# Seven block products in place of eight in the down projection of 12 of 16 feature groups, interleaved with the up projection

## The chip, the cores and the metric

One NeuronCore of one Trainium2 chip runs the whole program. The metric is the device time of one execution in microseconds; smaller is better. TensorE is called PE here (with PEld for its weight loads), VectorE DVE, ScalarE ACT, GpSimd POOL and SyncE SP.

## The reference, cut to what matters

The program is a decoder trunk of two layers on 256 tokens with 1024 model features, in float32. In each layer three attention branches are mixed and added to the residual stream x; that part is not touched. Then follows the MLP with 4096 hidden features:

```
h2 = RMSNorm(x, g_mlp)
x  = x + square(relu(h2 @ w_up)) @ w_down      # w_up 1024 x 4096, w_down 4096 x 1024
```

At the end stands a final RMSNorm of x.

## The kernel before, in words

**Numbers in two parts.** A float32 matrix product is made of three products of a shorter float format (float32r). Each operand is split into a high part (an ACT copy into that format) and a low part (a DVE subtraction, original minus high part, both inputs in SBUF). `split` (lines 84 to 93) does so for weights, with four buffers for each part (`whi`, `wlo`), 128x1024 at a time. `mm3` (117 to 121) issues the three matmuls high-high, high-low, low-high into one PSUM tile.

**Weights.** Every weight block comes by a DMA of 1 MB from the SP queue into one of four buffers `raw`, then goes through two splits. `w_cols` (111) brings 256 columns of all 1024 rows, `w_rows` (99) 512 rows of 512 columns.

**The MLP (665 to 726).** The 4096 hidden features are 16 groups of 256. The norm's factor per token is left out of the up product and put in at the end as its square (`r2`).
The up stage runs over the groups: for each of the two blocks of 128 features, eight steps over the model features, three matmuls each, with a weight block as the stationary operand and all 256 tokens as the moving one: 48 matmuls of 256 columns per group. Then `up_done` makes relu (ACT, from PSUM), the square (DVE, `max(o,0) * r`, one input from PSUM), the high part (ACT) and the low part (DVE), and the group stays in SBUF as `uh`, `ul` (a pair of tiles for each group).
The down stage runs after all 16 groups: `stream_tok` makes for each half of the output columns (`cg`, 512 columns) 32 steps over the hidden features, for each of the two token blocks `j`, three matmuls of 512 columns with an activation block 128x128 as the stationary operand. A group of 256 features takes 2 steps x 2 token blocks x 2 halves = 8 block products, 24 matmuls. The result in PSUM is scaled by r2 and added to x by DVE (line 713).
In layer 0 the transposes of x for the next layer's norm (`norm_in`, `part`) follow each half; in layer 1 the final norm and the output DMAs.

**Order.** PE's order is written out by hand from the attention output projection to the first two up groups (`tc.manual_schedule`, left at line 694). Everything else, on every engine, is put in order at build time by a planner that follows its own timing of the program; on the chip each engine then runs its list strictly in order, and an instruction that waits holds up those behind it. POOL has no work in the MLP but a few tiny operations for the norm.

**PSUM** has eight banks: three under the name mm, two at, two pt, one av.

Of the kernel before, what the change touches and what calls it, by code (L numbers as in the profile page):

```python
# [32 lines left out]
def trunk_kernel(ctx: ExitStack, tc: tile.TileContext, x, positions, g_mix, w_in, b_forget, w_branch,  # L33
                 w_out, g_mlp, w_up, w_down, g_final, out):
    nc = tc.nc
    act, dve, pool, pe, dma = nc.scalar, nc.vector, nc.gpsimd, nc.tensor, nc.sync
# [7 lines left out]
    def mm_tile(name="mm"):  # L44
        return ps.tile([128, 512], F32, name=name, tag="mm", bufs=3)
# [4 lines left out]
    def pt_tile(name="pt"):  # L50
        return ps.tile([128, 512], F32, name=name, tag="pt", bufs=2)
# [6 lines left out]
    xs = [[xh[h][:, j, :] for h in range(2)] for j in range(2)]  # L58
# [21 lines left out]
    mhalf = const.tile([128, 2], F32, name="mhalf")  # L80
    pool.memset(mhalf, -0.5)


    def split(raw, k, n, steps=1):
        hi = wp.tile([128, 1024], F32R, name="whi", tag="whi", bufs=4)
        lo = wp.tile([128, 1024], F32R, name="wlo", tag="wlo", bufs=4)
        h3 = hi[:, :k * n].rearrange("p (k n) -> p k n", k=k)
        l3 = lo[:, :k * n].rearrange("p (k n) -> p k n", k=k)
        m = k // steps
        for i in range(0, k, m):  # L90
            act.activation(h3[:, i:i + m], raw[:, i:i + m], AF.Copy)  # L91
# [19 lines left out]
    def w_cols(src, off, rs):  # L111

        raw = raw_tile(8, 256)
        dma.dma_start(raw, AP(src, off, [[rs, 128], [128 * rs, 8], [1, 256]]))
        return [split(raw[:, :, 128 * b:128 * b + 128], 8, 128) for b in range(2)]

    def mm3(o, a, b, start, stop):
        (ah, al), (bh, bl) = a, b
        pe.matmul(o, ah, bh, start=start, stop=False)  # L119
        pe.matmul(o, ah, bl, start=False, stop=False)  # L120
        pe.matmul(o, al, bh, start=False, stop=stop)  # L121
# [69 lines left out]
    def stream_tok(lhs, nk, src, off, rs, n, split_last=False):  # L191

        return stream_groups(lhs, nk, src, [(off, n)], rs, split_last)[0]
# [21 lines left out]
    for layer in range(DEPTH):  # L215
# [8 lines left out]
        with tc.tile_pool(name=f"att{layer}", bufs=1, reuse_waits="tile") as att:  # L224
# [21 lines left out]
            if layer == 0:  # L246
# [25 lines left out]
                for q in range(2):  # L272
                    dve.tensor_scalar(self_[32 * q:32 * q + 8, :], ident[32 * q:32 * q + 8, 32 * q:32 * q + 8], -1.0, None,
                                      op0=OP.mult)
# [13 lines left out]
                for s in range(2):  # L288
                    dve.tensor_scalar(nrev[:, :, s, :], ang[:, :, 0, :], 1.0 / TWO_PI, 0.25 * s, op0=OP.mult, op1=OP.add)
                dve.tensor_scalar(nrev, nrev, MAGIC, None, op0=OP.add)  # L290
                dve.tensor_scalar(nrev, nrev, MAGIC, None, op0=OP.subtract)
                dve.tensor_copy(ang[:, :, 1, :], ang[:, :, 0, :])
                p1 = 6.28125
                p2 = float(np.round((TWO_PI - p1) * 2.0 ** 21) / 2.0 ** 21)
                p3 = float(np.float32(TWO_PI - p1 - p2))
                for c in (p1, p2, p3):
                    dve.scalar_tensor_tensor(ang, nrev, -c, ang, op0=OP.mult, op1=OP.add)
                dve.tensor_scalar(ang[:, :, 1, :], ang[:, :, 1, :], float(np.float32(TWO_PI / 4)), None, op0=OP.add)
                lim = 3.1415925
# [10 lines left out]
            for c, nh in ((QI, 5), (QC, 10)):  # L310
                for j in range(2):
                    v = ct[:, j, c:c + nh * 64].rearrange("p (h d) -> p h d", h=nh)[:, :, 0:16]
                    v = v.rearrange("p h (a f) -> p h a f", a=2)
# [21 lines left out]
            for n, c in enumerate((KI, KC, KC + 64)):  # L335
# [3 lines left out]
                p = at_tile("kT")  # L339
                for j in range(2):  # L340
                    pe.transpose(p[:, j * 128:j * 128 + 128], kdup[:, j, n, :], ident)
                hi, lo = kh[:, n, :], kl[:, n, :]
# [12 lines left out]
            for j, c, n in SEG:  # L355
                for h in range(4):
                    z = at_tile("zi")
                    i = h % 2
                    qk2(z[:, :n], qi[:, h // 2, i, j * 128:j * 128 + 128], kh[:, 0, 0:n], kl[:, 0, 0:n])
                    r = att.tile([128, 256], F32, name="ri", tag="ri", bufs=2)  # L360
# [3 lines left out]
                                             op0=OP.mult, op1=OP.add)  # L364

            for j, c, n in SEG:
                s = sc[:, c:c + n]
                for r in range(TOPK // 8):
                    m8 = small.tile([128, 8], F32, name="m8")
                    dve.max(m8, s)  # L370
                    dve.match_replace(s, m8, s, GONE)
            mb = att.tile([128, 384], F32, name="mb", tag="mb", bufs=1)
# [42 lines left out]
            p = at_tile("cum")  # L415
# [10 lines left out]
            p = at_tile("cumt")  # L426
# [171 lines left out]
            for b in range(4):  # L598
# [5 lines left out]
                for c in (0, 256):  # L604
                    v = th[:, :, c:c + 128]
# [4 lines left out]
                                   op0=OP.mult, op1=OP.add)  # L610
# [14 lines left out]
            for b in range(4):  # L625
                zs = []
                for i in range(2):
                    z = at_tile("zb")
                    h = 2 * b + i
# [21 lines left out]
            pe_order = tc.manual_schedule(engines={mybir.EngineType.PE})  # L651
# [11 lines left out]


        with tc.tile_pool(name=f"mlp{layer}", bufs=1, reuse_waits="tile") as mlp:
            uT = []
            def up_done(o, hi, lo):
                n = 256 * hi.shape[1]
                r = mlp.tile([128, 512], F32, name="ur", tag="ur", bufs=2)[:, :n]
                act.activation(r, o, AF.Relu)  # L670
                dve.scalar_tensor_tensor(r, o, 0.0, r, op0=OP.max, op1=OP.mult)
                r3 = r.rearrange("p (b t) -> p b t", t=256)
                act.activation(hi, r3, AF.Copy)
                dve.tensor_sub(lo, r3, hi.bitcast(F32))

            def up_mm(o, wb, ks):
                h, l = wb
                for k in ks:
                    mm3(o, (h[:, k, :], l[:, k, :]), blk(xt, k), k == 0, k == 7)

            first = []
            for c in range(16):
                uT.append((mlp.tile([128, 2, 256], F32R, name=f"uh{c}"), mlp.tile([128, 2, 256], F32R, name=f"ul{c}")))
            for c in range(2):
                first += [((mm_tile, (mm_tile, av_tile)[n])[c](), w) for n, w in enumerate(w_cols(w_up, layer * D * DFF + c * 256, DFF))]
            for ks in (range(4), range(4, 8)):
                for n, (o, w) in enumerate(first):
                    up_mm(o[:, 0:256], w, ks)
                    if n == 0 and not ks[0]:
                        part(1)  # L690
                    if ks[0]:
                        hi, lo = uT[n // 2]
                        up_done(o[:, 0:256], hi[:, n % 2:n % 2 + 1, :], lo[:, n % 2:n % 2 + 1, :])
            pe_order.__exit__(None, None, None)
            for c in range(2, 16):
                o = mm_tile()
                for b, w in enumerate(w_cols(w_up, layer * D * DFF + c * 256, DFF)):
                    up_mm(o[:, b * 256:b * 256 + 256], w, range(8))
                up_done(o, *uT[c])
            rstd = rstd_of(ss)  # L700
            r2 = small.tile([128, 2], F32, name="r2")
            pool.tensor_mul(r2, rstd, rstd)
            last = layer == DEPTH - 1
            if last:
                gfb = mlp.tile([128, D], F32, name="gfb")
                dma.dma_start(gfb, AP(g_final, 0, [[0, 128], [1, D]]))
                ss = small.tile([128, 2, 2], F32, name="ss")
            else:
                xt, ss, part = norm_in(layer * 8 + 8, (at_tile, pt_tile))
            for cg in range(2):  # L710
                o = stream_tok(uT, 32, w_down, layer * DFF * D + cg * 512, D, 512, split_last=last and cg == 1)
                for j in range(2):
                    dve.scalar_tensor_tensor(xs[j][cg], o[j], r2[:, j:j + 1], xs[j][cg], op0=OP.mult, op1=OP.add)
                    if last:
                        junk = small.tile([128, 512], mybir.dt.bfloat16, name="junk", tag="junk", bufs=1)
                        act.activation(junk, xs[j][cg], AF.Square, accum_out=ss[:, j, cg:cg + 1])
                        dve.tensor_mul(xs[j][cg], xs[j][cg], gfb[:, cg * 512:cg * 512 + 512])
                if not last:
                    part(cg)
                for j in range(2):  # L720
                    if last and cg == 1:
                        rl = rstd_of(ss[:, j:j + 1, :])
                        act.activation(xs[j][1], xs[j][1], AF.Copy, scale=rl)
                        dma.dma_start(AP(out, j * 128 * D + 512, [[D, 128], [1, 512]]), xs[j][1])
                        dve.tensor_scalar(xs[j][0], xs[j][0], rl, None, op0=OP.mult)
                        dma.dma_start(AP(out, j * 128 * D, [[D, 128], [1, 512]]), xs[j][0])
# [23 lines left out]
```

## Time and profile before

| | |
|---|---|
| median of 3 runs | 889.51 us (888.76 to 890.77) |
| profiled execution | 889.98 us, span 888.3 us |
| busy PE / DVE / ACT / POOL | 873.0 / 621.6 / 531.1 / 113.9 us |
| instructions PE / DVE / ACT / POOL | 5342 / 1008 / 874 / 216 |
| moved by DMA | 150.97 MB, mean 170 GB/s |

The span runs from the first to the last instruction. Busy time of an engine adds up its instructions without counting an overlap twice. Matmuls overlap in a pipeline, so the pace of PE is read from the starts of matmuls that follow one another, not from the duration of one. A duration of DVE or POOL as the profile shows it contains time in which the instruction was held up after it had been issued.

### The profile page before, as it was taken

How to read it: one execution, taken by the hardware profiler on the slowest of the kernel's cores; microseconds unless marked ns; L12 is line 12 of the kernel's file. 1: busy time of each engine (PE TensorE's matmuls, PEld its weight loads, DVE VectorE, ACT ScalarE, POOL GpSimd, SP SyncE). 2: the span in 40 equal slices, each digit the busy share in tenths (PEclk: the TensorE clock that was granted, in tenths of full speed). 3: DMA queues.
4: the chain of work that ended last, by engine and by line, in shares of the span. 5: the costliest groups of instructions: out<-in, count | busy, mean ns of one | idle time of the engine just before them, and what ended most of it. 6: DMA issues, size and time to landing. Idle time of an engine off the chain costs nothing.

```text
span 888.3 us, 13911 instructions
## 1 busy us (share of the span) xinstructions
PE 873.0 (98%) x5342; PEld 789.1 (89%) x5342; DVE 621.6 (70%) x1008; ACT 531.1 (60%) x874; POOL 113.9 (13%) x216
## 2 busy tenths in 40 slices
PE   7999999999999999999999999999999999999996
PEld 7998998888889999888899989988888999998885
DVE  5899787978766666545468987789876676664552
ACT  6766886776455555444365758677755655553442
POOL 2300321234001000000011014022600100000001
PEclk9999999999999999999999999999999999999998
DMA  8744544354555555555466463453346555555521
GB/s 288 244 147 143 190 143 143 116 169 143 190 190 164 176 183 190 190 189 190 137 208 195 139 197 136 143 189 128 106 150 232 169 190 190 190 188 192 190 95 48
DMA packets 102482, 150.97 MB, mean 170 GB/s; under 512 B 2928, under 2 KB 58256, under 8 KB 102416
## 3 DMA queue, kind: packets, MB, share of 16 engines
q1 hardware_dynamic: 102416, 150.08, 51.5%
q8 instruction: 42, 0.69, 0.3%
q14 instruction: 24, 0.20, 0.1%
HBM read 149.02 MB, written 1.05 MB: 169 GB/s over the span
## 4 chain that ended last, share of the span: by engine, by line
PE 92%; DVE 4%; ACT 1%; DMA 1%; issue 1%; SPq 0%; POOL 0%; POOLq 0%; ACTq 0%
PE mm L120 26%; PE mm L119 26%; PE mm L121 26%; PE av L454 2%; PE pT L438 2%; PE at L120 1%; PE at L121 1%; PE at L119 1%; DVE wlo L92 1%; DVE qs L145 1%; PE xtp L168 1%; ACT qs L143 1%; DMA x<-in_x_dram 1%; PE za L347 0%; PE yTp L579 0%
## 5 line engine op out<-in xcount | busy, mean ns | idle before, releaser
L92 DVE TENSOR_TENSOR wlo<-raw,whi 128x1024 fp32r<-128x1024 f32 (+3 forms) x289 | 347.8, 1206 | 201.0 <-ACT whi L91 199.4
L91 ACT ACTIVATE whi<-raw 128x1024 fp32r<-128x1024 f32 (+3 forms) x289 | 298.5, 1036 | 253.1 <-PE mm L121 142.4
L121 PE MATMUL mm<-xTh,wlo 128*128 128x256 f32 x752 | 214.0, 285 | 0.0
L119 PE MATMUL mm<-xTh,whi 128*128 128x256 f32 x752 | 213.8, 284 | 0.0
L120 PE MATMUL mm<-xTl,whi 128*128 128x256 f32 x752 | 213.6, 284 | 0.0
L119 PEld LDWEIGHTS mm<-xTh,whi 128*128 128x128 f32 x752 | 144.2, 192 | 0.2
L120 PEld LDWEIGHTS mm<-xTl,whi 128*128 128x128 f32 x752 | 144.2, 192 | 0.2
L121 PEld LDWEIGHTS mm<-xTh,wlo 128*128 128x128 f32 x752 | 144.2, 192 | 0.0
L120 PE MATMUL mm<-wlo,xTh 128*128 128x512 f32 (+2 forms) x320 | 122.7, 384 | 0.5 <-DVE wlo L92 0.5
L121 PE MATMUL mm<-whi,xTl 128*128 128x512 f32 (+2 forms) x320 | 121.6, 383 | 0.0
L119 PE MATMUL mm<-whi,xTh 128*128 128x512 f32 (+2 forms) x320 | 119.4, 383 | 0.3 <-ACT xTh L173 0.3
L121 PE MATMUL mm<-whi,ul 128*128 128x512 f32 x256 | 99.7, 389 | 0.0
L120 PE MATMUL mm<-wlo,uh 128*128 128x512 f32 x256 | 99.6, 389 | 0.0
L119 PE MATMUL mm<-whi,uh 128*128 128x512 f32 x256 | 99.2, 389 | 0.0
L120 PEld LDWEIGHTS mm<-wlo,xTh 128*128 128x128 f32 x320 | 61.0, 191 | 10.3 <-DVE wlo L92 1.3
L119 PEld LDWEIGHTS mm<-whi,xTh 128*128 128x128 f32 x320 | 60.9, 190 | 10.2 <-ACT xTh L173 0.7
L121 PEld LDWEIGHTS mm<-whi,xTl 128*128 128x128 f32 x320 | 60.8, 190 | 9.0
L185 POOL TENSOR_TENSOR ms<-ss 128x2 f32<-128x2 f32 (+1 forms) x6 | 4.3, 718 | 474.4 <-ACT junk L178 297.7
L121 PEld LDWEIGHTS mm<-whi,ul 128*128 128x128 f32 x256 | 48.1, 188 | 10.0
L120 PEld LDWEIGHTS mm<-wlo,uh 128*128 128x128 f32 x256 | 48.1, 188 | 10.0
L119 PEld LDWEIGHTS mm<-whi,uh 128*128 128x128 f32 x256 | 48.1, 188 | 9.7
L487 POOL TENSOR_SCALAR e<-e,rs 128x128 f32<-128x128 f32 x64 | 43.2, 693 | 27.2 <-DVE rs L484 27.2
(215 smaller groups left out, 1274.0 us busy)
## 6 DMA issues: line engine op xcount, KB each, us to landing
raw<-in_w_in_dram SPq DMA_DIRECT2D x48, 1024.0 KB, 5.0
raw<-in_w_up_dram SPq DMA_DIRECT2D x32, 1024.0 KB, 5.1
raw<-in_w_down_dram SPq DMA_DIRECT2D x32, 1024.0 KB, 5.0
raw<-in_w_branch_dram SPq DMA_DIRECT2D x12, 1024.0 KB, 5.0
raw<-in_w_out_dram SPq DMA_DIRECT2D x8, 1024.0 KB, 5.0
raw<-in_w_in_dram SPq DMA_DIRECT2D x8, 736.0 KB, 5.4
raw<-in_w_in_dram SPq DMA_DIRECT2D x3, 728.0 KB, 4.3
out_dram<-x SPq DMA_DIRECT2D x4, 256.0 KB, 2.2
```

The lines of the kernel that those rows point to most:

```text
L91: act.activation(h3[:, i:i + m], raw[:, i:i + m], AF.Copy)
L92: dve.tensor_sub(l3[:, i:i + m], raw[:, i:i + m], h3[:, i:i + m].bitcast(F32))
L119: pe.matmul(o, ah, bh, start=start, stop=False)
L120: pe.matmul(o, ah, bl, start=False, stop=False)
L121: pe.matmul(o, al, bh, start=False, stop=stop)
L143: act.activation(dst[half(i), :, i, :], src[half(i)], AF.Copy, scale=scale)
L145: dve.scalar_tensor_tensor(dst[half(1 - i), :, i, :], src[half(i)], scale, dst[half(i), :, i, :].bitcast(F32), op0=OP.mult, op1=OP.subtract)
L168: pe.transpose(p[:, i * 256 + j * 128:i * 256 + j * 128 + 128], xs[j][h][:, c:c + 128], ident)
L185: pool.tensor_add(ms, ss[:, :, 0], ss[:, :, 1])
L438: pe.transpose(p[:, q * 128:q * 128 + 128], e[:, i, q * 128:q * 128 + 128], ident)
L454: pe.matmul(o[:, c + c0:c + 256], v, p[:, a:b], start=s == 0 and n == 0, stop=s == 1 and n == 1)
L487: pool.tensor_scalar(e[:, i, c:c + n], e[:, i, c:c + n], rs[:, i, j:j + 1], 1.0, op0=OP.mult, op1=OP.mult)
```

## The change

For 12 of the 16 groups (`NS = 12`) the group's down product is seen as a 2x2 by 2x2 block product: two token blocks by two feature blocks, times two feature blocks by two halves of the output columns. Seven products of sums and differences of blocks take the place of eight products of blocks.

- Left side, in `up_done`: relu goes from PSUM to SBUF, and the square is made of its copy (`tensor_mul`, both inputs in SBUF). Of the four squared blocks, sums and differences are made: two on DVE, two on POOL, 128x128 each. Seven blocks (128x896) are then split into high (ACT) and low (DVE). The tiles `fh`, `fl` have three buffers.
- Right side, in `down`: the 1 MB of w_down for the group comes as 256 rows of 1024 columns. POOL makes the four combinations T by three subtractions (two halves at once: 128x1024, then 128x512, 128x512). `split_cols` splits four pieces (128x512, then three of 128x1024) into high (ACT) and low (DVE), in tiles `sh`, `sl` with four buffers.
- The seven products are summed over the 12 groups in seven PSUM banks, all but one of pt, which the up products take.
- The loop alternates: up of group c, then down of group c - 2, for c from 2 to 13. PE's order is written out by hand to the end of this loop. r2 is made ahead of the loop.
- After it `down_sum` puts the seven sums together (two ACT copies from PSUM, five DVE and two POOL operations of 128x512), and four DVE operations add them to x. Groups 14 and 15 go up, and groups 12 to 15 go through `stream_tok` as before.

```diff
+    def split_cols(src, pl, tag, bufs):
...
+        act.activation(r[0], src, AF.Copy)
+        dve.tensor_sub(r[1], src, r[0].bitcast(F32))
...
+            def up_part(c, o, b, nb):
...
                 act.activation(r, o, AF.Relu)
-                dve.scalar_tensor_tensor(r, o, 0.0, r, op0=OP.max, op1=OP.mult)
-                r3 = r.rearrange("p (b t) -> p b t", t=256)
-                act.activation(hi, r3, AF.Copy)
-                dve.tensor_sub(lo, r3, hi.bitcast(F32))
+                dve.tensor_mul(sq[c][:, 2 * b:2 * b + 2 * nb], r.rearrange("p (s t) -> p s t", t=128),
+                               r.rearrange("p (s t) -> p s t", t=128))
+            def up_done(c):
...
+                    dve.tensor_add(u[:, 4], u[:, 0], u[:, 2])
+                    dve.tensor_sub(u[:, 6], u[:, 1], u[:, 0])
+                    pool.tensor_sub(u[:, 5], u[:, 4], u[:, 1])
+                    pool.tensor_sub(u[:, 7], u[:, 3], u[:, 5])
+                    hi, lo = [mlp.tile([128, 7, 128], F32R, name=f"f{t}", tag=f"f{t}", bufs=3) for t in "hl"]
+                    uT[c] = (hi, lo)
+                    v = u[:, 1:8]
+                act.activation(hi, v, AF.Copy)
+                dve.tensor_sub(lo, v, hi.bitcast(F32))
...
+            ORDER = ((1, 0), (2, 2), (3, 6), (5, 3), (7, 5), (6, 4), (4, 1))
+            def down(c):
+                raw = raw_tile(2, 1024)
+                dma.dma_start(raw, AP(w_down, (layer * DFF + c * 256) * D, [[D, 128], [128 * D, 2], [1, D]]))
+                r4 = raw.rearrange("p k (h n) -> p k h n", h=2)
+                t = mlp.tile([128, 4, 512], F32, name="T", tag="T", bufs=2)
+                pool.tensor_sub(t[:, 0:2], r4[:, :, 1, :], r4[:, 0])
...
+                for v in (r4[:, 0, 0, :], r4[:, 1], t[:, 0:2], t[:, 2:4]):
+                    h, l = split_cols(v, mlp, "s", 4)
...
+                    mm3(prod[p], (hi[:, f], lo[:, f]), w, c == 0, c == NS - 1)
...
-            pe_order.__exit__(None, None, None)
-            for c in range(2, 16):
-                o = mm_tile()
...
+            for c in range(2, NS + 2):
+                up(c, pt_tile())
+                down(c - 2)
+            pe_order.__exit__(None, None, None)
+            down_sum(r2)
+            for c in range(NS + 2, 16):
+                up(c, (pt_tile, mm_tile)[c % 2]())
...
-                o = stream_tok(uT, 32, w_down, layer * DFF * D + cg * 512, D, 512, split_last=last and cg == 1)
+                o = stream_tok([uT[c] for c in range(NS, 16)], 32 - 2 * NS, w_down, (layer * DFF + NS * 256) * D + cg * 512, D, 512, split_last=last and cg == 1)
```

## Rows read from the trace of the kernel before

**Rows 1.** The page's first part: busy us (share of the span) x instructions.
```profile
PE 873.0 (98%) x5342; PEld 789.1 (89%) x5342; DVE 621.6 (70%) x1008; ACT 531.1 (60%) x874; POOL 113.9 (13%) x216
```
**Rows 2.** The page's chain of work that ended last, by engine.
```profile
PE 92%; DVE 4%; ACT 1%; DMA 1%; issue 1%; SPq 0%; POOL 0%; POOLq 0%; ACTq 0%
```
**Rows 3.** Stretches: start:end, length, busy PE, PEld, DVE, ACT, POOL (instructions), clock, DMA.
```profile
265.00:278.00 13.00, 13.00 (x110) 12.96 (x109) 8.26 (x13) 8.16 (x15) 2.36 (x4) 1.00 0.35 118
278.00:358.00 80.00, 80.00 (x669) 80.00 (x669) 52.10 (x61) 43.89 (x59) 0.00 (x0) 1.00 0.59 191
358.00:445.00 87.00, 87.00 (x391) 72.11 (x390) 42.17 (x41) 36.79 (x42) 0.00 (x0) 1.00 0.55 177
```
**Rows 4.** Waits of PE, whole span: us in total, times, longest.
```profile
PE mm L120 <- DVE wlo L92: 0.5, 2, 0.3
```
**Rows 5.** Order of time, PE, up and down stage of layer 0: start, us.
```profile
320.05 0.28 PE L119 MATMUL mm<-xTh,whi 128*128 128x256 f32 x1
...
325.45 0.28 PE L119 MATMUL mm<-xTh,whi 128*128 128x256 f32 x1
...
360.28 0.39 PE L119 MATMUL mm<-whi,uh 128*128 128x512 f32 x1
...
363.00 0.39 PE L119 MATMUL mm<-whi,uh 128*128 128x512 f32 x1
```
**Rows 6.** Groups of instructions by shape, DVE: busy us, mean ns, idle before.
```profile
L92 DVE TENSOR_TENSOR wlo<-raw,whi 128x1024 fp32r<-128x1024 f32 x264 | 325.6, 1236 | 183.1 <-ACT whi L91 181.8
L674 DVE TENSOR_TENSOR ul<-ur,uh 128x512 fp32r<-128x512 f32 x28 | 19.2, 684 | 0.0
L674 DVE TENSOR_TENSOR ul<-ur,uh 128x256 fp32r<-128x256 f32 x8 | 3.3, 417 | 0.0
L713 DVE SCALAR_TENSOR_TENSOR x<-mm,r,x 128x512 f32<-128x512 f32 x8 | 5.7, 745 | 6.1 <-PE mm L121 6.1
```
**Rows 7.** The same view, ACT.
```profile
L91 ACT ACTIVATE whi<-raw 128x1024 fp32r<-128x1024 f32 x264 | 278.8, 1059 | 236.3 <-PE mm L121 131.7 <-PE mm L120 93.4 <-PE at L121 6.5
L673 ACT ACTIVATE uh<-ur 128x512 fp32r<-128x512 f32 x28 | 17.2, 615 | 0.0
L670 ACT ACTIVATE ur<-mm 128x512 f32<-128x512 f32 x28 | 16.2, 578 | 0.0
```
**Rows 8.** The same view, POOL, a sum of two SBUF inputs.
```profile
L320 POOL TENSOR_TENSOR ct<-rt,rt 128x160 f32<-128x160 f32 x4 | 2.2, 550 | 0.3
```
**Rows 9.** Order of time, DVE, 201.5 to 206.7 us (attention, layer 0): start, us.
```profile
202.01 0.67 DVE L566 SCALAR_TENSOR_TENSOR gate<-gate,mm 128x512 f32<-128x512 f32 x1
202.60 0.67 DVE L463 TENSOR_TENSOR k2l<-avs,k2h 128x256 fp32r<-128x256 f32 x1
...
203.80 1.72 DVE L92 TENSOR_TENSOR wlo<-raw,whi 128x1024 fp32r<-128x1024 f32 x1
...
205.97 1.79 DVE L92 TENSOR_TENSOR wlo<-raw,whi 128x1024 fp32r<-128x1024 f32 x1
```
**Rows 10.** The same stretch and view, POOL: three sums of two SBUF inputs.
```profile
201.70 1.29 POOL L567 TENSOR_TENSOR y<-y,gate 128x512 f32<-128x512 f32 x1 [0.58 <-DVE gate L566]
...
202.95 1.49 POOL L567 TENSOR_TENSOR y<-y,gate 128x512 f32<-128x512 f32 x1
...
204.39 2.29 POOL L567 TENSOR_TENSOR y<-y,gate 128x512 f32<-128x512 f32 x1
```
**Rows 11.** Order of time, DVE, with POOL idle: two splits together, and k2l.
```profile
265.99 2.35 DVE L92 TENSOR_TENSOR wlo<-raw,whi 128x1024 fp32r<-128x1024 f32 x2
...
212.48 0.41 DVE L463 TENSOR_TENSOR k2l<-avs,k2h 128x256 fp32r<-128x256 f32 x1
```
**Rows 12.** Stretch near the start, columns as in rows 3.
```profile
9.00:12.00 3.00, 2.33 (x11) 1.93 (x10) 1.37 (x4) 2.21 (x7) 0.24 (x2) 1.00 1.06 398
```

More of the change, by code (lines that the diff above doesn't have):

```diff
@@ L81, in trunk_kernel @@
     pool.memset(mhalf, -0.5)
+    def split_cols(src, pl, tag, bufs):
+        n = int(np.prod(src.shape[1:]))
+        r = []
+        for t in ("h", "l"):
+            w = pl.tile([128, 1024], F32R, name=tag + t, tag=tag + t, bufs=bufs)[:, :n]
+            r.append(w.rearrange("p (k n) -> p k n", k=src.shape[1]) if len(src.shape) == 3 else w)
+        act.activation(r[0], src, AF.Copy)
+        dve.tensor_sub(r[1], src, r[0].bitcast(F32))
+        return r
     def split(raw, k, n, steps=1):
@@ L665, in trunk_kernel @@
         with tc.tile_pool(name=f"mlp{layer}", bufs=1, reuse_waits="tile") as mlp:
[L666 to L669, printed above, removed]
-                act.activation(r, o, AF.Relu)
-                dve.scalar_tensor_tensor(r, o, 0.0, r, op0=OP.max, op1=OP.mult)
-                r3 = r.rearrange("p (b t) -> p b t", t=256)
-                act.activation(hi, r3, AF.Copy)
-                dve.tensor_sub(lo, r3, hi.bitcast(F32))
+            sq, uT = {}, {}
+            def up_part(c, o, b, nb):
+                if c not in sq:
+                    sq[c] = mlp.tile([128, 8, 128], F32, name="sq", tag="sq", bufs=2)
+                r = mlp.tile([128, 512], F32, name="ur", tag="ur", bufs=2)[:, :nb * 256]
+                act.activation(r, o, AF.Relu)
+                dve.tensor_mul(sq[c][:, 2 * b:2 * b + 2 * nb], r.rearrange("p (s t) -> p s t", t=128),
+                               r.rearrange("p (s t) -> p s t", t=128))
+            def up_done(c):
+                u = sq[c]
+                if c >= NS:
+                    hi, lo = [mlp.tile([128, 2, 256], F32R, name=f"u{t}{c}") for t in "hl"]
+                    uT[c] = (hi, lo)
+                    hi, lo = [t.rearrange("p b (j t) -> p (b j) t", j=2) for t in (hi, lo)]
+                    v = u[:, 0:4]
+                else:
+                    dve.tensor_add(u[:, 4], u[:, 0], u[:, 2])
[3 more added lines that the diff above has]
+                    hi, lo = [mlp.tile([128, 7, 128], F32R, name=f"f{t}", tag=f"f{t}", bufs=3) for t in "hl"]
+                    uT[c] = (hi, lo)
+                    v = u[:, 1:8]
+                act.activation(hi, v, AF.Copy)
+                dve.tensor_sub(lo, v, hi.bitcast(F32))
             def up_mm(o, wb, ks):
@@ L679, in up_mm, with up @@
                     mm3(o, (h[:, k, :], l[:, k, :]), blk(xt, k), k == 0, k == 7)
+            def up(c, o):
+                for b, w in enumerate(w_cols(w_up, layer * D * DFF + c * 256, DFF)):
+                    up_mm(o[:, b * 256:b * 256 + 256], w, range(8))
+                up_part(c, o, 0, 2)
+                up_done(c)
+            prod = {}
+            ORDER = ((1, 0), (2, 2), (3, 6), (5, 3), (7, 5), (6, 4), (4, 1))
[5 more added lines that the diff above has]
+                pool.tensor_sub(t[:, 0:2], r4[:, :, 1, :], r4[:, 0])
+                pool.tensor_sub(t[:, 2], r4[:, 1, 1, :], t[:, 0])
+                pool.tensor_sub(t[:, 3], t[:, 2], r4[:, 1, 0, :])
+                right = []
+                for v in (r4[:, 0, 0, :], r4[:, 1], t[:, 0:2], t[:, 2:4]):
+                    h, l = split_cols(v, mlp, "s", 4)
+                    right += [(h, l)] if len(v.shape) == 2 else [(h[:, i], l[:, i]) for i in range(2)]
+                for (p, f), w in zip(ORDER, right):
+                    if p not in prod:
+                        prod[p] = {1: mm_tile, 2: mm_tile, 3: mm_tile, 5: at_tile, 7: at_tile, 6: av_tile, 4: pt_tile}[p](f"p{p}")
+                    hi, lo = uT[c]
+                    mm3(prod[p], (hi[:, f], lo[:, f]), w, c == 0, c == NS - 1)
@@ new lines, in down_sum @@
+            def down_sum(r2):
+                a = mlp.tile([128, 4, 512], F32, name="T", tag="T", bufs=2)
+                b = mlp.tile([128, 4, 512], F32, name="T", tag="T", bufs=2)
+                act.activation(a[:, 0], prod[1], AF.Copy)
+                act.activation(a[:, 1], prod[5], AF.Copy)
+                dve.tensor_add(b[:, 0], a[:, 0], prod[2])
+                dve.tensor_add(a[:, 2], a[:, 0], prod[6])
+                pool.tensor_add(b[:, 2], a[:, 2], a[:, 1])
+                dve.tensor_add(a[:, 3], a[:, 2], prod[7])
+                pool.tensor_add(b[:, 3], a[:, 3], a[:, 1])
+                dve.tensor_sub(b[:, 1], a[:, 3], prod[4])
+                dve.tensor_add(b[:, 2], b[:, 2], prod[3])
+                for i, (j, cg) in enumerate(((1, 0), (0, 0), (1, 1), (0, 1))):
+                    dve.scalar_tensor_tensor(xs[j][cg], b[:, i], r2[:, j:j + 1], xs[j][cg], op0=OP.mult, op1=OP.add)
@@ L681, in trunk_kernel @@
             first = []
-            for c in range(16):
-                uT.append((mlp.tile([128, 2, 256], F32R, name=f"uh{c}"), mlp.tile([128, 2, 256], F32R, name=f"ul{c}")))
             for c in range(2):
@@ L691, in trunk_kernel @@
                     if ks[0]:
-                        hi, lo = uT[n // 2]
-                        up_done(o[:, 0:256], hi[:, n % 2:n % 2 + 1, :], lo[:, n % 2:n % 2 + 1, :])
-            pe_order.__exit__(None, None, None)
-            for c in range(2, 16):
-                o = mm_tile()
-                for b, w in enumerate(w_cols(w_up, layer * D * DFF + c * 256, DFF)):
-                    up_mm(o[:, b * 256:b * 256 + 256], w, range(8))
-                up_done(o, *uT[c])
+                        up_part(n // 2, o[:, 0:256], n % 2, 1)
+                        if n % 2:
+                            up_done(n // 2)
             rstd = rstd_of(ss)
```

1 line of the change is left out of this document (added).

## The prediction

> **What bounds the kernel now.** I read five views. The page's first part puts PE at 98% of the span, DVE at 70%, POOL at 13% [rows 1], and the chain of waits gives PE 92% [rows 2]; shares of the whole span can hide a stage with another limit, so the next view is the table of stretches. Each layer's MLP has an up stage (278 to 358 us in layer 0) and a down stage (358 to 445 us); in both PE is busy for every microsecond at a granted clock of 1.00, and DVE for 52.1 of 80 and 42.2 of 87 us [rows 3]. In the list of waits the largest one of PE on a weight split is 0.5 us in two instances [rows 4]. So the MLP runs at PE's pace, and that pace comes from the order of time: in the up stage 45 matmuls (256 columns) start between 320.05 and 325.45, 0.120 us each; in the down stage 12 (512 columns) between 360.28 and 363.00, 0.2267 us each [rows 5]. A feature group costs PE 48 matmuls up (two blocks of 128 features, eight steps, three products each) x 0.120 = 5.76 us up and 24 x 0.2267 = 5.44 us down, 11.20 us together.
>
> **What the change takes from PE.** Seven products in place of eight: 21 matmuls per group instead of 24, same shapes. 3 x 12 groups x 2 layers = 72 matmuls x 0.2267 = 16.3 us. A pass of the new loop (up of one group, down of one) is 5.76 + 21 x 0.2267 = 10.52 us of PE. It is earned only if the other engines deliver a group in 10.52 us.
>
> **What it adds, per pass.** Durations of DVE [rows 6]: 1.236 us for 128x1024, 0.684 for 512, 0.417 for 256; by their slope 1.10 for 896 and 0.28 for 128. DVE does two splits of the up weights and three of 1024 on the down side (the second row block, T0/T1, T2/T3), 5 x 1.236 = 6.18; the 512 split and the square, 2 x 0.684 = 1.37; the low part of the seven activation combinations (896), 1.10; one add and one subtract of 128, 0.57. Sum 9.22 us in ten instructions, where before a group took 4 x 1.236 + 2 x 0.684 = 6.3.
> ACT [rows 7]: 5 x 1.059, 0.615 for 512, about 0.95 for 896, 0.578 for the relu: 7.4 us. It stays under PE.
> POOL, idle in these stages so far [rows 3], gets the subtractions of T (1024, 512, 512) and two of 128. One of 512 that meets nobody takes 1.29 us [rows 10], one of 160 takes 0.55 [rows 8]: 2.1 ns per element, so 2.38 for 1024 and 0.48 for 128. 2.38 + 2.58 + 0.96 = 5.9 us.
> DMA: the same two megabytes per group, in more time than before; 191 GB/s here, 398 GB/s in the first microseconds [rows 3, 12]. Not a limit.
> Each engine by itself is below 10.52 us. Read that way the change gives its 16.3 us.
>
> **Why I don't read it that way.** Around 202 us POOL runs three sums of 512, inputs and output in SBUF, while DVE works, and the records interlock. DVE's k2l (two SBUF inputs) starts at 202.60 and takes 0.67 us [rows 9], alone 0.41 [rows 11]: held up 0.26, to 202.86, when the first POOL sum (from 201.70, 1.29 us) is 0.14 from its end [rows 10]. The weight split of 203.80 takes 1.72 in place of 1.236: held to 204.28, 0.16 before the second sum (from 202.95, 1.49 us) ends. The third sum (from 204.39) takes 2.29, 1.0 more than alone: it gets going at about 205.39, 0.13 before that split ends at 205.52. The split of 205.97 takes 1.79: held to 206.53, 0.15 before the third sum ends. Each blocks the other, and hands over about 0.14 us before its recorded end. The DVE instruction of 202.01, with one SBUF input and one from PSUM, keeps its 0.67 beside a POOL sum.
> The Trainium skill, "SBUF — State Buffer", section "SBUF: two separate sides", calls the pair of ports that both engines use an exclusive lock for a whole instruction, for DVE work with two SBUF inputs against POOL work that reads SBUF. The rows above agree, but for the last 0.14 us of each instruction; by the page's whole instructions the sum would be that of rival A.
>
> All ten DVE instructions of a pass have two SBUF inputs (the old square read PSUM; the new one reads the relu's copy twice), and all five of POOL have too. So they must go one after the other: 9.22 + 5.9 = 15.1 us by durations. Less the handovers: five POOL instructions have ten changes of engine at 0.14 = 1.4; five DVE to DVE changes at 0.06 (two splits back to back take 2.35 [rows 11], not 2.47) = 0.3. That leaves 13.4 us per pass. Lower bound: only the slopes, no fixed part, 7296 elements x 1.07 ns + 2304 x 2.13 = 12.7. Upper bound: 15.1, nothing overlapped. I take 13.4, since the 202 us rows show both the block and the handover, and keep both ends.
> All three stand above 11.20. PE would wait about 2.9 us in each pass, behind the low halves of the down weights: the next up's matmuls stand behind the waiting product in PE's written order, so nothing fills the gap. Excess over the old pass: 13.4 - 11.2 = 2.2 us, times 24 passes = 52.8 us (bounds 1.5 and 3.9: 36 and 94).
>
> **The edges of the loop.** Before it, in the first two up groups, DVE is busy for 8.26 of 13 us [rows 3], so T and splits of the first group can be made ahead: up to 4.7 us per layer, I take half, -5 us in all (0 to -9.5). After it, the recombination: five DVE operations of 512 (0.684) and four additions to x (0.747 [rows 6]), 6.4 us, with two ACT copies and two POOL sums. PE has up 14 and 15, 11.5 us, as cover; DVE must in that time also do one group's splits (2.47), the square and low part of group 14 (1.37) and the first split of the remaining down weights (1.24): 11.5. Even, or 2.5 late if group 14's splits are still to be done; I take 1 per layer, +2 us (0 to +5). The single buffer left for up's PSUM tile costs nothing: between two ups stand 4.76 us of down, the relu takes 0.58. Moving r2 ahead of the loop costs nothing, POOL is free then [rows 3]. The kernel's end is unchanged.
>
> **The sum.** The profiled execution took 889.98 us (span 888.3); 889.98 + 52.8 - 5 + 2 = 939.8. The median of the runs is 0.5 below it, so 939. Own range: 889.5 + 36 - 9.5 = 916 to about 960.
>
> **Rivals.**
> A. The pair goes for whole instructions, or every switch costs what the handover saves: 15.1 us per pass, 889.5 + 24 x 3.92 - 5 + 2 = 981. For it: in a queue of alternating instructions a missed turn costs a whole instruction. Against: four handovers of about 0.14 us above.
> B. Faster. The port is no limit, because POOL slips its work into DVE's free time and PE stays the bound: 889.5 - 16.3 + 3 (recombination) = 876. For it: every engine alone is under 10.52. It decides from the point where POOL's 5.9 us cost DVE less than about 2.3 us per pass (11.2 - 8.9, its 9.22 less 0.3). The rows of 202 us seem near it: 3.9 us of POOL work delayed DVE by 0.26 + 0.49 + 0.56 = 1.31, in the same share 2.0 for 5.9. Against: there three of the nine DVE instructions could collide, here all ten can, and DVE has 1.3 us of a 10.52 us pass free for 5.9 us of POOL.
> C. Order, not the port. The four buffers of the down splits hold exactly one group: the fourth split of the next group waits for the last product of this one, then 1.06 + 1.24 us of split; the square, behind it on DVE, waits for the next up and its relu, 5.76 + 0.58. DVE can stand still for 6.3 - 2.3 = 4.0 us unless other splits were put there; POOL can use part of it. At half lost, 15.4 per pass: 889.5 + 24 x 4.2 - 5 + 2 = 987. Against: the up splits have buffers for two groups.
> Granted clock: it was 1.00 at 9 to 12 us with PE busy for 2.33 of 3 us [rows 12], so gaps of this size needn't lower it.
>
> **Chances.** Forecast 0.55, A 0.15, C 0.13, B 0.12, and 0.05 for what I don't see (a clock that falls after all, little change). The range takes the forecast, A and C in, 908 to 990; the likeliest case alone 916 to 960. Within 0.2% is about what a measurement here can't tell from no change. Faster by more 0.13, within 0.02, slower by more 0.85.
>
> **What would show it.** In the changed profile: PE with 72 matmuls less, busy about 857 us (873 - 16), and new waits of PE on the low halves of the down weights, some 2 to 3 us per pass; a pass of 13 to 14 us between one relu and the next; splits on DVE near 1.7 us or longer instead of 1.24 inside the loop, and POOL's 512 subtractions near 2.3 instead of 1.29. DVE and POOL together (without the overlap) fill the loop. If splits keep 1.24 and PE still waits, it is C; if PE shows no waits and the pass is 10.5 us, B holds and the forecast is wrong, at the step that puts the two engines one after the other.

## The result, and the profile after

The changed kernel took 935.71 us (median, 935.38 to 935.77), the kernel before 889.13 us beside it: ratio 1.0523, 95% interval 1.0503 to 1.0544. Slower by 5.2%, where 939 us was forecast. The profiled execution took 935.67 us, its span is 934.0 us.

The page's first part [rows 1]:
```profile
PE 877.7 (94%) x5270; PEld 781.7 (84%) x5270; DVE 797.7 (85%) x1118; ACT 569.8 (61%) x922; POOL 341.6 (37%) x340
```
PE has its 72 matmuls less. DVE has 176 us more busy time, POOL 228 us more, and both figures hold time in which an instruction stood after it had been issued.

PE's waits over the whole span, us in total, times, longest [rows 4]:
```profile
PE p L132 <- DVE sl L93: 27.5, 28, 1.3
PE mm L132 <- DVE xTl L186: 7.6, 4, 2.2
...
PE p L133 <- DVE fl L706: 4.4, 2, 2.3
```
The product in `p` waits for `sl`, the low half of a weight piece of the down side, as forecast. The other two are at the start of each layer's MLP, in the first ups and in the first down product.

The MLP of layer 0 in stretches [rows 3]: the first two up groups, the loop, and a part of the down stage that was not changed (PE, PEld, DVE, ACT, POOL, clock, DMA):
```profile
263.88:283.90 20.02, 15.75 (x105) 14.93 (x104) 16.91 (x17) 10.92 (x18) 16.40 (x10) 0.83 0.38 127
283.90:434.38 150.48, 134.60 (x834) 117.89 (x834) 150.35 (x122) 81.55 (x99) 97.16 (x54) 0.98 0.50 169
434.38:467.00 32.62, 32.62 (x194) 28.91 (x193) 22.85 (x30) 15.71 (x23) 2.55 (x2) 1.00 0.39 123
```
In the loop DVE, not PE, is busy all the time. How it fills that time is seen in one pass, in order of time (start, us). DVE:
```profile
329.14 1.08 DVE L706 TENSOR_TENSOR fl<-sq,fh 128x896 fp32r<-128x896 f32 x1
330.14 5.67 DVE L104 TENSOR_TENSOR wlo<-raw,whi 128x1024 fp32r<-128x1024 f32 x2
335.73 1.77 DVE L686 TENSOR_TENSOR sq<-ur 128x512 f32<-128x512 f32 x1
337.43 0.68 DVE L93 TENSOR_TENSOR sl<-raw,sh 128x512 fp32r<-128x512 f32 x1
338.03 0.28 DVE L698 TENSOR_TENSOR sq<-sq 128x128 f32<-128x128 f32 x1
338.23 0.28 DVE L699 TENSOR_TENSOR sq<-sq 128x128 f32<-128x128 f32 x1
338.44 1.50 DVE L93 TENSOR_TENSOR sl<-raw,sh 128x1024 fp32r<-128x1024 f32 x1
339.86 2.61 DVE L93 TENSOR_TENSOR sl<-T,sh 128x1024 fp32r<-128x1024 f32 x2
342.39 1.08 DVE L706 TENSOR_TENSOR fl<-sq,fh 128x896 fp32r<-128x896 f32 x1
```
and POOL, first a subtraction ahead of the loop, then the same pass:
```profile
264.13 2.40 POOL L729 TENSOR_TENSOR T<-raw 128x1024 f32<-128x1024 f32 x1 [53.95 <-PE at L133]
...
329.30 3.20 POOL L729 TENSOR_TENSOR T<-raw 128x1024 f32<-128x1024 f32 x1 [2.30 <-DVE sl L93]
332.57 2.15 POOL L730 TENSOR_TENSOR T<-raw,T 128x512 f32<-128x512 f32 x1
334.80 2.15 POOL L731 TENSOR_TENSOR T<-T,raw 128x512 f32<-128x512 f32 x1
338.39 0.46 POOL L700 TENSOR_TENSOR sq<-sq 128x128 f32<-128x128 f32 x1 [1.44 <-DVE sq L698]
338.93 1.31 POOL L701 TENSOR_TENSOR sq<-sq 128x128 f32<-128x128 f32 x1
```
A pass is 342.39 - 329.14 = 13.25 us; nine passes (302.64 to 421.86) take 119.22 us, 13.25 each. The first four DVE instructions and the three subtractions of T (T0/T1, T2, T3) are one chain across two engines. T0/T1 that meets nobody ahead of it takes 2.40 (at 264.13 us): of its 3.20 it stands 0.80, until 330.10, when `fl` is 0.12 from its recorded end (330.22). It ends at 332.50. The two splits of up weights take 5.67 in place of 2.35: the first gets going at about 332.37, the second after T2, and so on to the square, 1.77 in place of 0.68, which runs when T3 ends at 336.95. From T0/T1 to the square each instruction of the one engine waits for one of the other.

The price by form over the whole span, beside [rows 6]:
```profile
L104 DVE TENSOR_TENSOR wlo<-raw,whi 128x1024 fp32r<-128x1024 f32 x216 | 333.2, 1553 | 60.2 <-ACT whi L103 59.0
...
L686 DVE TENSOR_TENSOR sq<-ur 128x512 f32<-128x512 f32 x28 | 40.1, 1433 | 0.0
```
The mean is 1553 ns in place of 1236 for a split of up or attention weights, and 1433 in place of about 684 for the square.

### The profile page after: what moved, and what is told of

Its sections match the earlier page's. It is cut to its first block, busy times and chain, and to the rows that moved or that the text cites. A ratio compares the mean times of both kernels' runs of the same rounds, so it can differ in the third digit from the quotient of the medians.

```text
span 934.0 us, 14079 instructions
## 1 busy us (share of the span) xinstructions
PE 877.7 (94%) x5270; PEld 781.7 (84%) x5270; DVE 797.7 (85%) x1118; ACT 569.8 (61%) x922; POOL 341.6 (37%) x340
## 5 line engine op out<-in xcount | busy, mean ns | idle before, releaser
L104 DVE TENSOR_TENSOR wlo<-raw,whi 128x1024 fp32r<-128x1024 f32 (+2 forms) x241 | 355.3, 1484 | 75.8 <-ACT whi L103 74.1
L103 ACT ACTIVATE whi<-raw 128x1024 fp32r<-128x1024 f32 (+2 forms) x241 | 245.3, 1028 | 129.1 <-PE mm L133 63.7
L133 PE MATMUL pt<-xTh,wlo 128*128 128x256 f32 x416 | 117.9, 283 | 0.0
L132 PE MATMUL pt<-xTl,whi 128*128 128x256 f32 x416 | 117.9, 283 | 0.0
L131 PE MATMUL pt<-xTh,whi 128*128 128x256 f32 x416 | 117.7, 283 | 0.0
L132 PE MATMUL mm<-xTl,whi 128*128 128x256 f32 x336 | 98.7, 294 | 7.6 <-DVE xTl L186 7.6
L133 PE MATMUL mm<-xTh,wlo 128*128 128x256 f32 x336 | 98.4, 293 | 0.0
L131 PE MATMUL mm<-xTh,whi 128*128 128x256 f32 x336 | 98.3, 293 | 0.0
L132 PEld LDWEIGHTS pt<-xTl,whi 128*128 128x128 f32 x416 | 79.8, 192 | 0.9
L131 PEld LDWEIGHTS pt<-xTh,whi 128*128 128x128 f32 x416 | 79.8, 192 | 1.0
```

## The experiments

Line numbers of the kernels below are those of the changed kernel or a few higher. A pass is read each time from one `fl` to the next.

**The port or the work: POOL reads nothing in the loop**
```diff
-                pool.tensor_sub(t[:, 0:2], r4[:, :, 1, :], r4[:, 0])
-                pool.tensor_sub(t[:, 2], r4[:, 1, 1, :], t[:, 0])
-                pool.tensor_sub(t[:, 3], t[:, 2], r4[:, 1, 0, :])
-                for v in (r4[:, 0, 0, :], r4[:, 1], t[:, 0:2], t[:, 2:4]):
+                for v in (r4[:, 0, 0, :], r4[:, 1], r4[:, 0], r4[:, 1]):
-                    pool.tensor_sub(u[:, 5], u[:, 4], u[:, 1])
-                    pool.tensor_sub(u[:, 7], u[:, 3], u[:, 5])
+                    pool.memset(u[:, 5], 0.0)
+                    pool.memset(u[:, 7], 0.0)
```
The five subtractions of POOL are left out (raw blocks and zeros stand in their place). Every instruction of PE, DVE and ACT stays, but the planner put DVE's list in a slightly other order (one split of a down piece now stands ahead of those of the up weights).


> The five POOL subtractions of a pass are left out (the T pieces are replaced by blocks of w_down as they came, two activation combinations by a memset), so the products are not those of the reference; PE, DVE and ACT do as much as before. Port theory (DVE and POOL instructions with SBUF reads go one after the other, 13.25 us per pass): without POOL's reads DVE needs about 9 us, PE's 10.5 us decide, 889.1 - 16.3 plus 0 to 6 for the edges = 873 to 880 us. Order theory (four split buffers, DVE's list): buffers and list stay, so the pass stays near 13 us, above 920. DVE's own work as the bound (its records fill the whole loop): its ten instructions stay, near 935.


876.61 us against 888.2, ratio 0.9869 (0.9837 to 0.9901). The pass is 341.63 - 331.10 = 10.53 us, PE's own 10.52. Two `fl`, then the loop in a table of stretches:
```profile
331.10 1.08 DVE L706 TENSOR_TENSOR fl<-sq,fh 128x896 fp32r<-128x896 f32 x1
...
341.63 1.09 DVE L706 TENSOR_TENSOR fl<-sq,fh 128x896 fp32r<-128x896 f32 x1
```
```profile
300.00:420.00 120.00, 120.00 (x795) 110.71 (x794) 94.76 (x111) 74.59 (x87) 5.02 (x16) 1.00 0.56 185
```
PE is full and DVE has 25 of 120 us free. Of 935.7 us, 59 are the price of POOL's subtractions; without them the kernel is as fast as rival B priced it (876). PE's busy time is 856.4 us here, with the same 5270 matmuls as after the change.

**The same work on the engine that looks full: the subtractions on DVE**
```diff
-                pool.tensor_sub(t[:, 0:2], r4[:, :, 1, :], r4[:, 0])
+                dve.tensor_sub(t[:, 0:2], r4[:, :, 1, :], r4[:, 0])
-                pool.tensor_sub(t[:, 2], r4[:, 1, 1, :], t[:, 0])
+                dve.tensor_sub(t[:, 2], r4[:, 1, 1, :], t[:, 0])
...
```


> The five subtractions move from POOL to DVE, the engine whose records already fill the loop. Port theory: a subtraction holds the port for 1.07 ns per element on DVE in place of 2.1 on POOL, so a pass takes 8.5 + 2.8 = 11.3 us in place of 13.25: 935.7 - 24 x 1.95 = 889 (883 to 895). DVE's own work as the bound: 2.8 us more per pass, 935.7 + 67 = 1003. Order theory: no gain, 930 to 1000.


893.41 us, ratio 1.0054 (1.0031 to 1.0077). Pass 339.73 - 328.70 = 11.03 us. DVE, busy for 797.7 us with POOL's help, is busy for 754.5 without it. Two `fl` and the loop:
```profile
328.70 1.08 DVE L706 TENSOR_TENSOR fl<-sq,fh 128x896 fp32r<-128x896 f32 x1
...
339.73 1.08 DVE L706 TENSOR_TENSOR fl<-sq,fh 128x896 fp32r<-128x896 f32 x1
```
```profile
300.00:420.00 120.00, 118.77 (x778) 107.60 (x777) 118.38 (x158) 75.74 (x88) 2.56 (x2) 1.00 0.53 185
```
DVE took on five more instructions in a shorter pass, so DVE's own work was not the bound. The buffers of the splits are as before, so too few of them (part of rival C) is not it either. An order of work is not ruled out by this run alone, since the planner put DVE's list in another order here too; the runs below keep that order. Most passes take 11.03 us; four early ones of layer 1 take 12.2 to 17.4, and its loop 133.5 us (715.97 to 849.51) where layer 0's takes 129.5 (281.55 to 411.02). Why was not tried.

**One input of the square from PSUM again**
```diff
-                dve.tensor_mul(sq[c][:, 2 * b:2 * b + 2 * nb], r.rearrange("p (s t) -> p s t", t=128),
-                               r.rearrange("p (s t) -> p s t", t=128))
+                dve.scalar_tensor_tensor(sq[c][:, 2 * b:2 * b + 2 * nb], o.rearrange("p (s t) -> p s t", t=128), 0.0,
+                                         r.rearrange("p (s t) -> p s t", t=128), op0=OP.max, op1=OP.mult)
```


> The square reads the product from PSUM again (max(o, 0) * r), one SBUF input in place of two, same DVE time. Port theory: 0.58 us per pass can lie beside a POOL subtraction, 935.7 - 24 x 0.58 = 922 (914 to 930). DVE's own work, or its order, as the bound: no change, 933 to 938, or a little slower because the PSUM tile of the up product is held longer.


930.46 us, ratio 1.0475 (1.0439 to 1.0511). In the pass the square is 0.68 long beside POOL's T3, and the pass 338.00 - 325.38 = 12.62, 0.63 less, as expected (0.58); DVE's order of work is that of the changed kernel. T3 on POOL and the square on DVE:
```profile
331.04 2.13 POOL L731 TENSOR_TENSOR T<-T,raw 128x512 f32<-128x512 f32 x1
331.97 0.68 DVE L686 SCALAR_TENSOR_TENSOR sq<-pt,ur 128x512 f32<-128x512 f32 x1
```
The total, 5 us less, fell short of the 14 expected and lies just outside the range. Only 18 of the 24 passes are of the steady kind (below), 18 x 0.63 = 11, and 6 are lost elsewhere. PE's waits show a new one:
```profile
PE pt L131 <- DVE sq L686: 25.4, 18, 1.9
```
The square now holds the up product's PSUM tile until DVE comes to it. So PE waits ahead of an up product and no longer in the middle of a down product, and has more left to do when DVE is through with the last steady pass. From the last `fl` of the passes to the first matmul of group 14, first here, then in the changed kernel:
```profile
413.81:429.69 15.88, 15.88 (x97) 14.20 (x97) 13.37 (x16) 9.98 (x13) 0.00 (x0) 1.00 0.56 199
```
```profile
421.86:434.02 12.16, 12.16 (x77) 11.02 (x76) 12.12 (x15) 9.43 (x13) 0.00 (x0) 1.00 0.67 244
```
That is 3.7 us more per layer, 7 in all, which covers the missing 6. It is read from the traces and was not tested by itself.

**More POOL reads: one more subtraction of 512 per pass**
```diff
+                scratch = mlp.tile([128, 512], F32, name="scratch", tag="scratch", bufs=1)
+                pool.tensor_sub(scratch, r4[:, 0, 0, :], r4[:, 1, 0, :])
```


> One more POOL subtraction of 128x512 per pass, of two raw blocks into a scratch tile that nobody reads. POOL was busy for 37% of the span. Port theory: it holds the port for about 1.13 us of each pass, 935.7 + 24 x 1.13 = 963 (955 to 968). Any theory in which POOL is off the path: 934 to 938.


962.05 us, ratio 1.0831 (1.0799 to 1.0862). Pass 336.62 - 322.29 = 14.33, 1.08 more: 1.29 less two handovers, roughly. DVE and POOL:
```profile
322.29 1.08 DVE L706 TENSOR_TENSOR fl<-sq,fh 128x896 fp32r<-128x896 f32 x1
...
336.62 1.08 DVE L706 TENSOR_TENSOR fl<-sq,fh 128x896 fp32r<-128x896 f32 x1
```
```profile
333.83 1.78 POOL L733 TENSOR_TENSOR scratch<-raw 128x512 f32<-128x512 f32 x1 [0.44 <-DMA raw<-in_w_down_dram]
336.78 3.19 POOL L729 TENSOR_TENSOR T<-raw 128x1024 f32<-128x1024 f32 x1 [1.17 <-DVE sl L93]
```
This is the run that leaves least room for another cause: DVE's work and its order are those of the changed kernel, nobody waits for the scratch tile, and POOL still stands free for 1.17 us behind the extra subtraction, so it does not make T late. It costs the pass its own time all the same. Too few buffers or the order of DVE's list (rival C), or a chain of POOL's work that comes late, would have left the pass as it was.

**More POOL work that reads nothing**
```diff
+                scratch = mlp.tile([128, 1024], F32, name="scratch", tag="scratch", bufs=1)
+                pool.memset(scratch, 0.0)
```


> As the run with one more POOL subtraction, but with a POOL memset of 128x1024, which writes SBUF and reads nothing and keeps POOL for about 1.1 us of a pass. Port theory, if the port is that of reads: no change, 933 to 939. If POOL's time as such counts, or its writes take part: 935.7 + 24 x 1.1 = 962.


942.97 us, ratio 1.0603 (1.0583 to 1.0622), outside the 933 to 939 and inconclusive: the pass kept its 13.25 us, but the memsets wait for nothing, the planner put them ahead of the passes, and the time was lost at the start of the loop. So once more, with the memset into the tile that the subtractions then fill, which ties it to its pass:
```diff
+                pool.memset(t[:, 2:4], 0.0)
                 pool.tensor_sub(t[:, 0:2], r4[:, :, 1, :], r4[:, 0])
```


> A POOL memset of 128x1024 per pass once more, this time into the half of T that the second and third subtraction write afterwards, so that it has to lie in its pass and ahead of the subtractions (the memset into a scratch tile lay outside the passes, so it told nothing of a pass). Port theory, with a port of reads: the pass stays 13.25 us. If POOL's writes or its time as such count: about 14.3 us per pass, 958 or more.


937.74 us, ratio 1.0546 (1.0528 to 1.0565); pass 343.28 - 330.04 = 13.24. POOL, in order of time:
```profile
330.17 0.96 POOL L729 MEMSET T<- 128x1024 f32 x1 [2.28 <-DVE sl L93]
331.09 3.44 POOL L730 TENSOR_TENSOR T<-raw 128x1024 f32<-128x1024 f32 x1
```
The memset lies beside `fl` (from 330.04), which keeps its 1.08 us. Like the extra subtraction it lies in time in which POOL was free, but it leaves the pass as it was. In the pass POOL's time as such costs nothing; its reads of SBUF do. The Trainium skill, "SBUF — State Buffer", section "Who interferes with whom", says that DVE work with two SBUF inputs contends with POOL work that reads SBUF and not with POOL work that only writes there: the subtraction (a pass of 14.33 us) and the memset (13.24) bear out both halves.

**Toward a faster version: fewer groups by seven products, subtractions on DVE**

With the subtractions on DVE a pass costs 11.03 us, more than PE's 10.52, so some ordinary up groups (PE 5.76, DVE 3.84) must stand among the passes. Two kernels, with 8 and with 10 groups; the diff is that of 8, with 10 the ordinary ups 10 to 13 stand in the passes of groups 2, 5, 8 and 9:
```diff
-NS = 12
+NS = 8
...
+            plain = {0: 8, 1: 9, 3: 10, 5: 11, 6: 12, 7: 13}
...
+                down_mm(c, right, 0, 4)
+                if c in plain:
+                    up(plain[c], pt_tile())
+                down_mm(c, right, 4, 7)
```


> Eight groups of 16 by seven products in place of 12, the subtractions on DVE, and the up products of the other groups spread over the passes between the two halves of a down product (two are left for the time after the loop), so that PE has 107 us in the loop of a layer against about 102 us of DVE. Port theory: PE decides, 889.1 - 8 x 2 x 0.68 = 878.2, plus 0 to 5 for the edges: 878 to 883. If the order of the lists or the recombination decides: 886 or more.

> As the run before with ten groups by seven products: PE 116.7 us in the loop of a layer, DVE 117.7. Port theory: both about even, 889.1 - 13.6 + 2 x 1 plus 0 to 6 for the edges: 877 to 884. If the order of the lists decides: 888 or more.


Both missed: 896.33 us, 1.008 (1.0066 to 1.0094), and 889.88, 1.0009 (0.9999 to 1.002). The first in stretches at the start of its loop:
```profile
280.00:290.00 10.00, 5.95 (x42) 5.22 (x41) 10.00 (x19) 4.46 (x6) 0.00 (x0) 0.94 0.70 220
```
DVE is full and PE stands: the first down product comes before DVE has made the last combination of the activations (ended at 286.90), whose high part `fh` PE waits 3.4 us for, and 0.6 more for `fl`. Next, T of groups 0 and 1 and the pieces of group 0 were held back until the last block of xT is made, so that they no longer run ahead of it, and one ordinary up was put ahead of the first down product (with 10 groups group 10, the others in the passes of groups 4, 8 and 9):
```diff
+                if c < 2:
+                    dve.tensor_copy(t[:, 0, 0:1], xt[3][1][:, 1, 0:1].bitcast(F32))
...
+            early, plain = {0: 8}, {1: 9, 3: 10, 5: 11, 6: 12, 7: 13}
```


> As the kernel with eight groups and the subtractions on DVE, but the first T and the first high parts wait for the last block of the transposed x, and one more up product stands ahead of the first down product. Theory: what that kernel lost against its 878 us lay in the first 35 us of each MLP, where T and splits made ahead of time stood in front of the low parts of x on DVE and PE's clock fell behind the gap; without that 878 to 885. If the loss lies elsewhere: 890 or more.

> The same repair of the start with ten groups by seven products. PE 116.7 us in the loop of a layer, DVE 115 by the pace of 11.03 us per pass that was measured with the subtractions on DVE. Theory: 889.1 - 13.6 plus 2 to 8 = 878 to 884. If the loss lies elsewhere: 888 or more.


Missed again: 889.97, 1.0017 (1.0008 to 1.0026), and 893.81, 1.0053 (1.0039 to 1.0067). With 8 groups the stretches put the loss in two places:
```profile
284.00:294.00 10.00, 6.64 (x46) 5.78 (x46) 9.10 (x15) 5.26 (x7) 0.00 (x0) 1.00 0.77 257
294.00:304.00 10.00, 10.00 (x69) 9.23 (x68) 9.54 (x15) 6.53 (x8) 0.00 (x0) 1.00 0.44 151
304.00:320.00 16.00, 14.76 (x108) 13.77 (x107) 15.45 (x20) 9.01 (x12) 0.00 (x0) 1.00 0.57 194
```
PE stands 3.4 + 1.2 = 4.6 us in layer 0, against 5.4 saved (8 x 3 x 0.2267), mostly for `fh` and `fl` of the first group. So DVE was still behind, and two or three ups were put ahead; the diff is that of two, with three the last line reads (8, 9, 10) and {4: 11, 6: 12, 7: 13}:
```diff
-            early, plain = {0: 8}, {1: 9, 3: 10, 5: 11, 6: 12, 7: 13}
+            early, plain = {0: (8, 9)}, {2: 10, 4: 11, 6: 12, 7: 13}
```


> Eight groups by seven products (saving 8 x 3 x 0.2267 = 5.44 us of PE per layer), subtractions on DVE, and two ordinary up groups instead of one ahead of the first down product, plain ups in the passes of groups 2, 4, 6, 7. In the kernel with one up ahead PE stood about 4.6 us per layer (3.4 between 284 and 294 us, 1.2 between 304 and 320) because DVE was behind with the first group's low parts. One more up ahead is 5.76 us of PE against 3.84 of DVE, 1.9 us more cover. Theory (DVE's backlog at the start is what eats the saving): 4.6 - 1.9 = 2.7 us lost per layer, 889.1 - 10.9 + 5.4 + 1 = 885, range 882 to 888. Rival (the saving goes elsewhere, for instance into passes without an ordinary up, where DVE's 11 us exceed PE's 10.5): 889 to 892, PE's waits moved to later passes.

> The same with three ordinary up groups ahead of the first down product, and plain ups only in the passes of groups 4, 6 and 7. Theory: 4.6 - 3.8 = 0.8 us left of the start's loss per layer, 889.1 - 10.9 + 1.6 + 1 = 881; four passes in a row without an ordinary up cost up to 4 x 0.5 us per layer, so 881 to 885. Rival: 889 to 892, as above.


Two ahead: 886.38 us, ratio 0.9968 (0.9956 to 0.9981), inside its 882 to 888 and 0.3% faster than the kernel before. Three ahead: 897.36, 1.0095 (1.008 to 1.0109), against 881 to 885. First the stretches with two, then with three:
```profile
264.00:284.00 20.00, 19.40 (x163) 19.20 (x162) 17.02 (x25) 13.78 (x25) 2.37 (x4) 1.00 0.54 175
284.00:294.00 10.00, 9.72 (x80) 9.28 (x78) 10.00 (x17) 6.12 (x7) 0.00 (x0) 1.00 0.72 242
```
```profile
264.00:284.00 20.00, 20.00 (x170) 20.00 (x169) 15.59 (x28) 13.62 (x25) 2.36 (x4) 1.00 0.53 172
...
320.00:360.00 40.00, 33.95 (x206) 30.18 (x205) 36.58 (x53) 21.82 (x26) 0.00 (x0) 0.91 0.49 164
```
With two, 3.4 us of PE's waits are left in layer 0 and 2.6 in layer 1, of 10.9 saved. The spans of the two profiles differ by 888.3 - 883.2 = 5.1, but about half of that is not the MLP's: layer 0's MLP starts at 262.58 here and at 265.19 before, behind a part that the edits do not touch (262.6 to 265.4 in the traces of this case). The MLPs themselves are shorter by 0.8 us in layer 0 (262.58 to 442.79 against 265.19 to 446.20) and by 1.8 in layer 1 (last matmul 178.1 us behind the first, in place of 179.9). That agrees with the medians, 888.83 - 886.38 = 2.5. With three, DVE stands free for 4.4 of the first 20 us because its down work begins later, and PE, which ran ahead, waits 6.0 us between 320 and 360, most of it (5.5) for `fh` of a later group. That is read from the trace and was not tested by itself.

## Why the prediction was right, point by point

- **PE's saving** (72 matmuls, a pass of 10.52): right. The kernel without POOL's reads runs at 10.53 per pass. The waits are a little smaller than the 2 to 3 us per pass: in a steady pass PE stands for up to 2.1 us, and its matmuls take 11.14 where 10.52 was reckoned.
- **One after the other, 13.4 us per pass**: 13.25 measured. The lone durations add to 9.1 + 5.9 = 15.0 (T0/T1 2.40, T2 and T3 1.29, u5 0.46, u7 about 0.5), and the handovers take off 1.8, where 1.7 was worked out. The hand-over of 0.14 us read at 202 us [rows 9, 10] is 0.12 to 0.13 here. POOL's reads taken away, moved, or added to moved the pass by -2.72, -2.22 and +1.08.
- **Rival A** (15.1) and **B** (10.5) are out by the pass; **C** is out because DVE has no free time in the loop and because one more subtraction on POOL, with DVE's list in the same order, made the pass 1.08 us longer.
- **Excess of 2.2 us in 24 passes, +52.8**: mis-sized. Nine passes per layer run at 13.25, 2.05 over 11.2, +18.5. PE's loop runs from 283.97 to 434.02, 150.1 us, so the other three take 150.1 - 119.2 = 30.8 us, 2.8 less than three old passes: T and pieces for the first groups were already made, and in the last (421.86 to 434.38) POOL has nothing to do. Together +15.7 per layer (150.1 against 12 x 11.2, and 150.2 in layer 1), where 26.4 was predicted.
- **The start, a credit of 2.5 per layer**: the step that failed, with the wrong sign. The first two ups took 20.1 us (263.88 to 283.97) where they took 12.4 (265.19 to 277.57), and 19.9 in layer 1: +7.6. The matmuls at these times, before and after:
```profile
265.19 0.28 PE L119 MATMUL mm<-xTh,whi 128*128 128x256 f32 x1
...
277.57 0.28 PE L119 MATMUL mm<-xTh,whi 128*128 128x256 f32 x1
```
```profile
263.88 0.28 PE L131 MATMUL mm<-xTh,whi 128*128 128x256 f32 x1
...
283.97 0.28 PE L131 MATMUL pt<-xTh,whi 128*128 128x256 f32 x1
```
 DVE's free time there was real, but the planner put the first group's T and pieces ahead of the low parts of xT and of the up weights, and on the shared pair. The stretches:
```profile
272.00:274.00 2.00, 0.86 (x3) 0.48 (x3) 2.00 (x3) 1.16 (x2) 1.84 (x3) 1.00 1.01 410
274.00:276.00 2.00, 0.02 (x1) 0.00 (x0) 2.00 (x4) 0.47 (x1) 1.47 (x2) 0.72 1.01 311
276.00:278.00 2.00, 1.81 (x8) 1.81 (x9) 0.52 (x2) 0.00 (x0) 1.96 (x1) 0.50 0.67 236
278.00:280.00 2.00, 2.00 (x12) 2.00 (x11) 0.82 (x1) 1.33 (x2) 1.89 (x2) 0.50 0.00 0
```
 PE stands almost still from 272 to 276, waiting for `xTl`, and then works at a granted clock of 0.50 (1.2 GHz) until about 281.5. Most of the 7.6 us goes with POOL's reads: without them, but with DVE's share of the early work left in, the two ups take 14.0 us (262.97 to 276.97).
- **The tail, +1 per layer**: nothing. From the first matmul of group 14 to the end of layer 0's MLP pass 34.3 us (434.02 to 468.29), and the same work took 34.2 before (two ups 11.5, four groups' down products 21.8, the transposes of x about 0.9).
- **The sum**: per layer 15.7 + 7.6 = 23.3 measured against 26.4 - 2.5 + 1 = 24.9. Two errors of about 10 us, one each way, so the total is nearer than its terms. The shorter first passes and the longer start belong together: work was done earlier. Of the ranges, the upper end of 960 and the lower end of 908 follow from no term of the sum.
- **"Gaps of this size needn't lower the clock"**: wrong. It was 0.50 after the gap above and in some passes, at 340 to 342 us for instance:
```profile
340.00:342.00 2.00, 2.00 (x5) 1.61 (x6) 2.00 (x2) 1.72 (x2) 0.24 (x1) 0.50 0.42 95
```
 In the loop it cost nothing that shows, since DVE sets the pass; at the start, five microseconds at half clock delayed the ups by some 2.5 us. Together with the gaps themselves it is why PE's busy time is 877.7 us and not the 857 predicted: the kernel with the same matmuls and hardly a gap shows 856.4, and a pass with waits has PE busy for 11.14 us even at a clock of 1.00 (below).

What stays open: about 1 us per layer of the kernels with one and with two ups ahead, which PE's idle time does not explain, and the longer loop in layer 1 of the kernel with the subtractions on DVE.

## What to carry to other kernels

Before work is given to POOL because it is idle, look at the operands on both sides: if DVE's instructions have two SBUF inputs and POOL's read SBUF, add the two engines' times as if they were one engine. In that case the full engine may well be the better place: five subtractions moved from POOL to DVE brought the pass from 13.25 to 11.03 us. And work made ahead of a loop is not free because an engine has gaps there: what counts is what it delays on that engine, from its queue or from the other engine under the lock, here the low parts that the first matmuls wait for.

## What the runs showed of the hardware that was not expected

- The busier engine can be the better place. POOL is nearly twice as slow per element as DVE on the same subtraction, as the prediction had it: 2.40 us for 128x1024 against 1.22, 1.29 for 128x512 against 0.68. Under the lock, that is why the move to DVE pays: 5.9 us on POOL become 3.1 on DVE.
- A granted clock of 0.50 followed four microseconds in which PE was busy for 0.88 us (272 to 276). Passes in which PE stood for 2.1 of 13.25 us showed it too, but not each of them; the first of these two did for a part, the second did not:
```profile
329.14:342.39 13.25, 11.15 (x66) 9.55 (x65) 13.25 (x12) 6.70 (x9) 9.28 (x5) 0.90 0.48 159
395.38:408.62 13.24, 11.14 (x70) 9.54 (x69) 13.24 (x12) 6.70 (x9) 9.28 (x5) 1.00 0.48 158
```
